# Differential-attention scores of an encoder layer on 64 contraction rows at a time, with one reduction per map

## Chip, cores and metric

One core of one Trainium2 chip runs the whole layer. The metric is the device time of one execution in microseconds (us), the median of several runs.

## What is computed

The reference is one encoder layer in float32: a norm, a wide input projection, a state-space mixer, a differential attention with 8 heads, two gates, an output projection and a feed-forward block. The change touches the scores of the attention:

```python
def one_block(args):
    qb, qpos = args
    bucket = _rel_bucket(k_pos[None, :] - qpos[:, None])
    bias = jnp.transpose(rel_table[bucket], (2, 0, 1)).astype(jnp.float32)
    s = jnp.einsum('bqhtd,bkhtd->bhtqk', qb, k,
                   preferred_element_type=jnp.float32) * scale + bias[None, :, None]
    p = jax.nn.softmax(s, axis=-1)
    w = p[:, :, 0] - lam32 * p[:, :, 1]
    return jnp.einsum('bhqk,bkhe->bqhe', w.astype(v.dtype), v)
```

There are 1024 queries, 1040 keys (16 of them from the meta tokens), 8 heads, and in each head two maps (the index t) whose head dimension is 64.

## The kernel before

Every float32 operand of a large product is split into two parts, hi and lo (`split`, line 87), and most products are made of three partial products (`mm3`, line 91): hi by hi, lo by hi, hi by lo. The program is written in a manual order, so each engine runs its instructions in the order in which the code issues them, and an instruction that waits holds up all that follow it on its engine.

The attention stage works through 64 items (8 heads by 8 query tiles of 128). Each has two maps, so there are 128 maps of 128 queries by 1040 keys. Two items make a pair. For one map the steps are these, with the names that the order tables use (m is the map, a or b the item of the pair):

- `C`, function `sc_mm`, lines 1163 and 1164, on TensorE: the keys are taken in three chunks of 352, 344 and 344 columns. The stationary operands `qa` and `qb` hold hi and lo of 64 dimensions, one above the other, in 128 rows; K holds hi above lo. `qa` by K gives hi·hi + lo·lo, `qb` by K gives the two cross terms. A chunk writes a tile `S` of its own; the pool `pps` has four of them.
- `c`, function `sc_tt`, line 1175, on VectorE: one custom instruction per chunk adds the bias table `Tb`, writes the sum to `E` and keeps a running minimum in `mn`. The second and third chunk start from the `mn` that the chunk before left, and each instruction is followed by a short one that reads the accumulator out.
- `exp` (line 1181, ScalarE), `coef` (lines 1187 and 1188, VectorE), `comb` (lines 1195 to 1198, GpSimd: the two maps become one weight matrix `w`).
- `T` (line 1204, TensorE: transposes of `w` into the PSUM tile `wt`, two of which exist), `hi` (line 1214, ScalarE) and `lo` (line 1218, VectorE: the split of the transposed weights), `PV` (line 1239, TensorE: weights by V).

Beside these, each step of the loop carries a piece of the gated linear unit of the state-space branch (`GLU`, function `glu_mm`, 12 products through lines 92 to 94 into tile `f` or `o`), a transpose and a square for the norm of the attention output (`sqT`, `sq`), and small norm steps on VectorE (`n`, lines 1268 to 1280, through `mul` at line 85). The strings `RAMP`, `STEPS` and `TAIL` (lines 1473 to 1493) are the order, written out by hand: `STEPS` is one step of the steady loop (line 1572), a list of names, each with the number of steps by which its pair lags. Loads are issued on the SP queue by `load_head` and `load_q` once per head.

```python
nc.tensor.matmul(ps[:, 0:n], qa[:, qs], k, start=True, stop=False)
nc.tensor.matmul(ps[:, 0:n], qb[:, qs], k, start=False, stop=True)
```

Of the kernel before, what the change touches and what calls it, by code (L numbers as in the profile page):

```python
# [46 lines left out]
def _f(ap):  # L47
    return ap.bitcast(F32)
# [3 lines left out]
def tile_hybrid_encoder(ctx, tc, A, out, dbg=None, stop=None):  # L52
# [973 lines left out]
    HT = {}  # L1026

    def load_q(h, p):

        if h >= H:  # L1030
            return
        c = slice(512 * p, 512 * p + 512)
        for m in range(2):
            qa, qb = [kq.tile([128, 512], F32R, tag=f"Q{z}{m}", name=f"Q{z}{m}", bufs=2) for z in range(2)]
            d = slice(64 * m, 64 * m + 64)
            for z in range(2):
                o = slice(64 * z, 64 * z + 64)
                nc.sync.dma_start(_f(qa[o]), qd[h, z, d, c])
                nc.sync.dma_start(_f(qb[o]), qd[h, 1 - z, d, c])
            HT.setdefault(h, {})["Q", p, m] = qa, qb  # L1040

    def load_head(h):
        if h >= H:
            return
        K = [kq.tile([128, L], F32R, tag=f"K{m}", name=f"K{m}_{h}") for m in range(2)]
        Tb = kq.tile([128, 896 + L], F32, tag="Tb", name=f"Tb{h}")
        load_q(h, 0)
        for m in range(2):
            for z in range(2):
                nc.sync.dma_start(_f(K[m][64 * z:64 * z + 64]), kd[h, z, 64 * m:64 * m + 64, :])  # L1050

        tr = td[h, 0:1]
        nc.sync.dma_start(Tb, bass.AP(tr.tensor, tr.offset, [[1, 128], [1, 896 + L]]))
        HT[h].update(K=K, Tb=Tb)

# [42 lines left out]
    def open_s():  # L1098

        nonlocal pps  # L1100
        PP["c"].close()
        pps = pS.enter_context(tc.tile_pool(name="pps", bufs=4, space=PSUM, side="right"))
# [44 lines left out]
    CH = ((0, 352), (352, 344), (696, 344))  # L1147

    def sc_mm(i, m, c):
# [8 lines left out]
        c0, n = CH[c]  # L1158
        ps = IT[i]["S", m, c] = pps.tile([128, 352], F32, tag="S", name="S")
        qs = slice(128 * (qt % 4), 128 * (qt % 4) + 128)  # L1160
        k = hd["K"][m][:, c0:c0 + n]
        qa, qb = hd["Q", qt // 4, m]
        nc.tensor.matmul(ps[:, 0:n], qa[:, qs], k, start=True, stop=False)  # L1163
        nc.tensor.matmul(ps[:, 0:n], qb[:, qs], k, start=False, stop=True)  # L1164

    def sc_tt(i, m, c):
# [3 lines left out]
        if c == 0:  # L1170
            t["E", m] = ptl(ep, f"E{m}", [128, L], F32, 2)
        c0, n = CH[c]
        mn = t["mn"][:, m:m + 1]
        b0 = 128 * qt + c0
        V.tensor_tensor_reduce(out=t["E", m][:, c0:c0 + n], in0=t.pop(("S", m, c))[:, 0:n],  # L1175
                               in1=HT[h]["Tb"][:, b0:b0 + n], scale=1.0,
                               scalar=mn if c else 3.0e38, op0=ALU.add, op1=ALU.min, accum_out=mn)
# [289 lines left out]
    def c_step(u, c, t):  # L1467
# [5 lines left out]
    RAMP = ("X C01a@0 C00a@0 c00a@0 c01a@0 S C10b@0 S C10a@0 c10a@0 G S G N0 C02a@0 c02a@0 exp0a@0 S S H C12a@0 "  # L1473
# [8 lines left out]
    TAIL = ("c02b@31 c lo0b@30 sqT@29 exp0b@31 lo1b@30 coefb@31 sqa@29 T2b@30 sqb@29 combb@31 PV0y@30 PV0z@30 tanh "  # L1482
# [5 lines left out]
    STEPS = ("c02b:2 lo0b:3 C11a:1 sqT:4 C12a:1 lo1b:3 c10a:1 exp0b:2 c11a:1 C00a:1 sqa:4 T2b:3 coefb:2 C01a:1 "  # L1488
# [5 lines left out]
    ACTS = {}  # L1494
    for x in range(2):
        s_ = "ab"[x]
        for m in range(2):
            ACTS[f"exp{m}{s_}"] = lambda p, m=m, x=x: ex_map(2 * p + x, m)
            for c in range(3):
                ACTS[f"C{m}{c}{s_}"] = lambda p, m=m, c=c, x=x: sc_mm(2 * p + x, m, c)  # L1500
                ACTS[f"c{m}{c}{s_}"] = lambda p, m=m, c=c, x=x: sc_tt(2 * p + x, m, c)
# [29 lines left out]
    LC = max(lag for n, lag in order if n[0] in "Cc" and n[1] in "01")  # L1531
# [593 lines left out]
```

## Time and profile before

| | |
|---|---|
| median of 3 runs | 1905.64 us (1902.81 to 1908.32) |
| the profiled execution | 1903.11 us, of which the span of its instructions is 1900.9 us |
| PE, PEld, DVE busy over the span | 96 %, 86 %, 67 % |
| ACT, POOL busy over the span | 46 %, 46 % |
| mean granted clock of TensorE | 0.989 |
| the attention stage | scores from 637.8 to 1068.1 us |

PE is TensorE's matrix multiply, PEld its weight load, DVE is VectorE, ACT ScalarE, POOL GpSimd. A row of a group gives line, engine, operation, output and inputs, the shape, the count, the busy time, the mean length of one and the idle time of the engine just before. A matmul's length in the records includes the time through the array, so records of matmuls that follow one another overlap; the distance between their starts is what one of them costs the engine.

### The profile page before, as it was taken

How to read it: one execution, taken by the hardware profiler on the slowest of the kernel's cores; microseconds unless marked ns; L12 is line 12 of the kernel's file. 1: busy time of each engine (PE TensorE's matmuls, PEld its weight loads, DVE VectorE, ACT ScalarE, POOL GpSimd, SP SyncE). 2: the span in 40 equal slices, each digit the busy share in tenths (PEclk: the TensorE clock that was granted, in tenths of full speed). 3: DMA queues.
4: the chain of work that ended last, by engine and by line, in shares of the span. 5: the costliest groups of instructions: out<-in, count | busy, mean ns of one | idle time of the engine just before them, and what ended most of it. 6: DMA issues, size and time to landing. Idle time of an engine off the chain costs nothing. (4 is left out here: it accounts for less than half of the span.)

```text
span 1900.9 us, 31037 instructions
## 1 busy us (share of the span) xinstructions
PE 1827.6 (96%) x11306; PEld 1642.2 (86%) x11306; DVE 1268.6 (67%) x2601; ACT 867.9 (46%) x1597; POOL 871.6 (46%) x803
## 2 busy tenths in 40 slices
PE   8998999899999989999999899999999999999999
PEld 7997888889999889999999888998788887888887
DVE  6699997763544688989999864369554545654543
ACT  4324343233433367777767632234555554433332
POOL 3068999643332177777767500005765652400000
PEclk8999999999999999999999999999999999999999
DMA  7423323337678565454554346431644448986563
GB/s 218 121 76 86 99 89 109 99 103 235 234 245 290 199 172 148 128 155 140 154 145 143 108 161 219 133 117 56 214 146 157 148 156 304 345 282 202 183 210 116
DMA packets 230535, 315.89 MB, mean 166 GB/s; under 512 B 39560, under 2 KB 140472, under 8 KB 230344
## 3 DMA queue, kind: packets, MB, share of 16 engines
q1 hardware_dynamic: 209952, 283.14, 47.1%
q10 hardware_dynamic: 20432, 30.78, 4.4%
q8 instruction: 89, 1.46, 0.3%
q14 instruction: 62, 0.51, 0.1%
HBM read 212.28 MB, written 99.48 MB: 164 GB/s over the span
## 5 line engine op out<-in xcount | busy, mean ns | idle before, releaser
L89 DVE TENSOR_TENSOR fp<-fr,fp 128x1024 fp32r<-128x1024 f32 x112 | 141.1, 1306 | 128.0 <-ACT fp L88 127.4
L92 PE MATMUL ps<-wh,hnh 128*128 128x256 f32 x768 | 221.3, 288 | 4.7 <-DVE qraw L969 3.5
L93 PE MATMUL ps<-wh,hnl 128*128 128x256 f32 x768 | 219.1, 285 | 4.6 <-DVE hnl L89 4.6
L94 PE MATMUL ps<-wl,hnh 128*128 128x256 f32 x768 | 218.8, 285 | 0.0
L88 ACT CAST fp<-fr 128x1024 fp32r<-128x1024 f32 x112 | 110.4, 1050 | 180.8 <-PE pf L94 159.2
L94 PE MATMUL pf<-fp 128*128 128x512 f32 x448 | 174.5, 390 | 1.3 <-DVE fp L89 1.3
L92 PE MATMUL pf<-fp 128*128 128x512 f32 x448 | 174.5, 390 | 0.5 <-ACT fp L88 0.4
L93 PE MATMUL pf<-fp 128*128 128x512 f32 x448 | 174.3, 389 | 0.0
L1181 ACT ACTIVATE E<-E,st 128x1040 f32<-128x1040 f32 x128 | 149.4, 1167 | 47.4 <-DVE st L1175 37.7
L1175 DVE CUSTOM_DVE_ANT_0 E<-S,Tb,st 128x344 f32<-128x344 f32 x256 | 146.7, 574 | 27.1 <-PE S L1164 5.7
L1197 POOL TENSOR_TENSOR w<-E,E 128x1040 f32<-128x1040 f32 x64 | 155.4, 2427 | 5.3
L92 PEld LDWEIGHTS ps<-wh,hnh 128*128 128x128 f32 x768 | 147.7, 192 | 6.9 <-DVE qraw L969 4.1
L93 PEld LDWEIGHTS ps<-wh,hnl 128*128 128x128 f32 x768 | 147.8, 192 | 4.9 <-DVE hnl L89 4.8
L94 PEld LDWEIGHTS ps<-wl,hnh 128*128 128x128 f32 x768 | 148.0, 193 | 0.0
L1163 PE MATMUL S<-K,Q 128*128 128x344 f32 (+1 forms) x384 | 134.5, 351 | 3.1 <-issue 3.0
L92 PE MATMUL ps<-hnh,wh 128*128 128x512 f32 (+2 forms) x352 | 133.6, 380 | 0.0
L93 PE MATMUL ps<-hnh,wl 128*128 128x512 f32 (+2 forms) x352 | 132.3, 376 | 1.3 <-POOL wl L174 1.0
L94 PE MATMUL ps<-hnl,wh 128*128 128x512 f32 (+2 forms) x352 | 131.4, 373 | 0.0
L89 DVE TENSOR_TENSOR swl<-w1r,swh 128x512 fp32r<-128x512 f32 x70 | 79.6, 1167 | 70.4 <-ACT swh L88 70.3
L1214 ACT CAST W<-wt 128x384 fp32r<-128x384 f32 x192 | 89.3, 481 | 79.3 <-PE wt L1204 71.6
L1164 PE MATMUL S<-K,Q 128*128 128x344 f32 (+1 forms) x384 | 123.5, 323 | 0.0
L1195 POOL TENSOR_SCALAR E<-E,st 128x1040 f32<-128x1040 f32 x64 | 74.4, 1163 | 97.1 <-DVE st L1188 55.3
(428 smaller groups left out, 5328.4 us busy)
## 6 DMA issues: line engine op xcount, KB each, us to landing
fr<-ad SPq DMA_DIRECT2D x56, 512.0 KB
ad<-r SPq DMA_DIRECT2D x91, 256.0 KB
raw<-in_w_in_dram SPq DMA_DIRECT2D x44, 512.0 KB
w<-in_w_ff_dram SPq DMA_DIRECT2D x32, 512.0 KB
wd<-w SPq DMA_DIRECT2D x32, 512.0 KB
Q<-qd SPq DMA_DIRECT2D x128, 128.0 KB
fr<-wd SPq DMA_DIRECT2D x32, 512.0 KB
w1r<-in_w_ff_dram SPq DMA_DIRECT2D x28, 512.0 KB
```

The lines of the kernel that those rows point to most:

```text
L88: nc.scalar.copy(hi, src)
L89: (eng or nc.vector).tensor_tensor(out=lo, in0=src, in1=_f(hi), op=ALU.subtract)
L92: nc.tensor.matmul(o, l[0], r[0], start=start, stop=False, **kw)
L93: nc.tensor.matmul(o, l[1], r[0], start=False, stop=False, **kw)
L94: nc.tensor.matmul(o, l[0], r[1], start=False, stop=stop, **kw)
L1163: nc.tensor.matmul(ps[:, 0:n], qa[:, qs], k, start=True, stop=False)
L1164: nc.tensor.matmul(ps[:, 0:n], qb[:, qs], k, start=False, stop=True)
L1175: V.tensor_tensor_reduce(out=t["E", m][:, c0:c0 + n], in0=t.pop(("S", m, c))[:, 0:n], in1=HT[h]["Tb"][:, b0:b0 + n], scale=1.0, scalar=mn ...
L1181: nc.scalar.activation(t["E", m], t["E", m], AF.Exp, bias=t["mn"][:, m:m + 1], scale=-1.0, accum_out=t["Z"][:, m:m + 1])
L1195: nc.gpsimd.tensor_scalar(out=E1, in0=E1, scalar1=t["cf"][:, 0:1], scalar2=0.0, op0=ALU.mult, op1=ALU.add)
L1197: nc.gpsimd.tensor_tensor(out=w[:, 112:], in0=_rev(E0), in1=_rev(E1), op=ALU.add)
L1214: nc.scalar.copy(WT[p, g][:, :, 0, x], IT[i]["tp", g])
```

## The change

The scores of a map are no longer two products over 128 rows but three over 64 rows, for two halves of the keys. Rows 0 to 63 of K hold the first 520 keys, rows 64 to 127 the last 520, in both cases hi in the first 520 columns and lo in the next 520. `qa` now holds hi in both halves of its rows and `qb` lo. A group of 260 keys gets three matmuls (hi·hi, lo·hi, hi·lo; the lo·lo term is left out), each on 64 rows and 260 columns; the groups of the upper and the lower rows alternate, so that consecutive matmuls use different halves of the array. A map has four groups and twelve matmuls. Its scores fill one tile of four banks, of which `pps` now has one instead of four small ones. VectorE runs one instruction over 1040 columns per map instead of three. K's loads read the same bytes in rows of 520 elements. `RAMP`, `STEPS` and `TAIL` are written anew; all twelve matmuls of a map now stand together.

```diff
+    NC = L // 4
@@ load_q
-                nc.sync.dma_start(_f(qa[o]), qd[h, z, d, c])
-                nc.sync.dma_start(_f(qb[o]), qd[h, 1 - z, d, c])
+                nc.sync.dma_start(_f(qa[o]), qd[h, 0, d, c])
+                nc.sync.dma_start(_f(qb[o]), qd[h, 1, d, c])
@@ load_head
-                nc.sync.dma_start(_f(K[m][64 * z:64 * z + 64]), kd[h, z, 64 * m:64 * m + 64, :])
+                nc.sync.dma_start(_f(K[m][64 * z:64 * z + 64]).rearrange("p (y n) -> p y n", y=2),
+                                  kd[h, :, 64 * m:64 * m + 64, 2 * NC * z:2 * NC * z + 2 * NC].rearrange("y p n -> p y n"))
@@ open_s
-        pps = pS.enter_context(tc.tile_pool(name="pps", bufs=4, space=PSUM, side="right"))
+        pps = pS.enter_context(tc.tile_pool(name="pps", bufs=1, space=PSUM, side="right"))
@@ sc_mm
-        c0, n = CH[c]
-        ps = IT[i]["S", m, c] = pps.tile([128, 352], F32, tag="S", name="S")
+        if c == 0:
+            IT[i]["S", m] = pps.tile([128, 4, 512], F32, tag="S", name="S")
+        if c % 2:
+            return
         qs = slice(128 * (qt % 4), 128 * (qt % 4) + 128)
-        k = hd["K"][m][:, c0:c0 + n]
         qa, qb = hd["Q", qt // 4, m]
-        nc.tensor.matmul(ps[:, 0:n], qa[:, qs], k, start=True, stop=False)
-        nc.tensor.matmul(ps[:, 0:n], qb[:, qs], k, start=False, stop=True)
+        for n, (q, y) in enumerate(((qa, 0), (qb, 0), (qa, 1))):
+            for z in range(2):
+                o = slice(64 * z, 64 * z + 64)
+                k0 = 2 * NC * y + NC * (c // 2)
+                nc.tensor.matmul(IT[i]["S", m][:, 2 * z + c // 2, 0:NC], q[o, qs], hd["K"][m][o, k0:k0 + NC],
+                                 start=n == 0, stop=n == 2)
@@ sc_tt
+        E = t["E", m] = ptl(ep, f"E{m}", [128, L], F32, 2)
+        b0 = 128 * qt
+        V.tensor_tensor_reduce(out=E.rearrange("p (c n) -> p c n", c=4), in0=t.pop(("S", m))[:, :, 0:NC],
+                               in1=HT[h]["Tb"][:, b0:b0 + L].rearrange("p (c n) -> p c n", c=4), scale=1.0,
+                               scalar=3.0e38, op0=ALU.add, op1=ALU.min, accum_out=t["mn"][:, m:m + 1])
@@ STEPS (first line of eight)
-    STEPS = ("c02b:2 lo0b:3 C11a:1 sqT:4 C12a:1 lo1b:3 c10a:1 exp0b:2 c11a:1 C00a:1 sqa:4 T2b:3 coefb:2 C01a:1 "
+    STEPS = ("C10a:1 C11a:1 C12a:1 C13a:1 lo0b:3 lo1b:3 sqT:4 exp0b:2 c1a:1 sqa:4 T2b:3 coefb:2 sqb:4 tanh:2 "
```

How the order moves is seen at two places of the steady loop. The first is TensorE, from the end of one group of PV products (line 1239 before, 1244 after the change) over a map of scores; K and Q are the operands of one map, `wt` the transposed weights. Before:

```order
L1163 MATMUL S<-K_5_10811,Q_10819 128x352 [waits DVE_49]
L1164 MATMUL S<-K_5_10811,Q_10820 128x352
L1163 MATMUL S<-K_5_10811,Q_10819 128x344 [waits DVE_49]
L1164 MATMUL S<-K_5_10811,Q_10820 128x344
L1204 MATMUL wt<-idn,w_7405 128x128 [waits DVE_49]
L1204 MATMUL wt<-idn,w_7405 128x128 x2
L1239 MATMUL o<-W,VV 128x256 x9
L1163 MATMUL S<-K_5_10811,Q_10819 128x344 [waits DVE_49]
L1164 MATMUL S<-K_5_10811,Q_10820 128x344
L1239 MATMUL o<-W,VV 128x256 [waits Activation_49]
```

With the change:

```order
L1244 MATMUL o<-W,VV 128x256 [waits Activation_49]
L1244 MATMUL o<-W,VV 128x256 x3
L1171 MATMUL S<-K_4_10172,Q_10575 128x260 [waits DVE_49]
L1171 MATMUL S<-K_4_10172,Q_10575 128x260
L1171 MATMUL S<-K_4_10172,Q_10576 128x260 x2
L1171 MATMUL S<-K_4_10172,Q_10575 128x260 x4
L1171 MATMUL S<-K_4_10172,Q_10576 128x260 x2
L1171 MATMUL S<-K_4_10172,Q_10575 128x260 x2
L1244 MATMUL o<-W,VV 128x256 x5
```

The six matmuls of a map, which stood in two or three places with transposes and PV products between them, have become a block of twelve that opens with a wait for VectorE.

The second place is VectorE over two maps of scores; `W` is the split of the transposed weights. Before:

```order
L1175 ISA E_10786,st<-S,Tb_10056 128x352 [waits PE_49]
L1175 ISA st 128x1
L1175 ISA E_10786,st<-S,Tb_10056,st 128x344 [waits DVE_49,PE_49]
L1175 ISA st 128x1
L1175 ISA E_10786,st<-S,Tb_10056,st 128x344 [waits DVE_49,PE_49]
L1175 ISA st 128x1
L1218 TENSOR_TENSOR W<-wt,W 128x3x128 [waits Activation_49] x2
L1175 ISA E_10842,st<-S,Tb_10056 128x352 [waits Pool_49]
```

With the change:

```order
L1180 ISA E_11298,st<-S,Tb_10961 128x1040 [waits PE_49,Pool_49]
L1180 ISA st 128x1
L1223 TENSOR_TENSOR W<-wt,W 128x3x128 [waits Activation_49]
L1180 ISA E_11338,st<-S,Tb_10961 128x1040 [waits PE_49]
L1180 ISA st 128x1
L1223 TENSOR_TENSOR W<-wt,W 128x3x128 [waits Activation_49] x2
L1180 ISA E_11392,st<-S,Tb_10961 128x1040 [waits PE_49,Pool_49]
```

Three instructions with two waits on VectorE's own earlier result have become one, which waits for all twelve matmuls of its map.

## Rows read from the trace of the kernel before

**Rows 1.** Busy time of each engine in the steady part of the attention stage.

```profile
core 0: us, PE busy (x) PEld busy (x) DVE busy (x) ACT busy (x) POOL busy (x), PEclk, DMA share, GB/s
700.00:1075.00 375.00, 357.35 (x2753) 348.50 (x2752) 337.73 (x1109) 268.80 (x604) 272.34 (x224) 0.99 0.49 142
760.00:1040.00 280.00, 265.82 (x2041) 259.27 (x2041) 254.44 (x828) 198.52 (x446) 202.31 (x166) 0.99 0.50 146
```

**Rows 2.** Who waited for whom, TensorE alone, 700 to 1075 us: total, times, longest.

```profile
PE wt L1204 <- DVE W L1218: 12.6, 7, 2.1
PE ot L1253 <- DVE W L1218: 4.8, 7, 1.0
PE S L1163 <- issue: 0.2, 1, 0.2
```

**Rows 3.** Groups of instructions by line from 760 to 1040 us.

```profile
L1175 DVE CUSTOM_DVE_ANT_0 E<-S,Tb,st 128x344 f32<-128x344 f32 x174 | 100.0, 574 | 18.8 <-PE S L1164 3.7
L1163 PE MATMUL S<-K,Q 128*128 128x344 f32 (+1 forms) x261 | 91.1, 350 | 0.0
L1164 PE MATMUL S<-K,Q 128*128 128x344 f32 (+1 forms) x262 | 84.0, 322 | 0.0
L1239 PE MATMUL o<-W,VV 128*128 128x256 f32 x519 | 78.1, 286 | 0.0
...
L1204 PE MATMUL wt<-idn,w 128*128 128x128 f32 x390 | 61.3, 274 | 10.8 <-DVE W L1218 10.8
...
L92 PE MATMUL f<-yTh,wh 128*128 128x256 f32 x172 | 51.4, 299 | 0.0
...
L1175 DVE CUSTOM_DVE_ANT_0 E<-S,Tb 128x352 f32<-128x352 f32 x87 | 44.9, 517 | 0.0
```

**Rows 4.** Timeline of TensorE: start, length, instruction.

```profile
963.55 0.28 PE L92 MATMUL f<-yTh,wh 128*128 128x256 f32 x1
...
964.97 0.32 PE L1163 MATMUL S<-K,Q 128*128 128x344 f32 x1
...
965.60 0.32 PE L1163 MATMUL S<-K,Q 128*128 128x352 f32 x1
...
974.61 0.49 PE L1204 MATMUL wt<-idn,w 128*128 128x128 f32 x3
```

**Rows 5.** Timeline of VectorE over one map.

```profile
962.94 0.52 DVE L1175 CUSTOM_DVE_ANT_0 E<-S,Tb 128x352 f32<-128x352 f32 x1
963.38 0.08 DVE L1175 DVE_READ_ACCUMULATOR2_ANT st<- 128x1 f32 x1
963.50 0.58 DVE L1175 CUSTOM_DVE_ANT_0 E<-S,Tb,st 128x344 f32<-128x344 f32 x1
...
964.23 0.58 DVE L1175 CUSTOM_DVE_ANT_0 E<-S,Tb,st 128x344 f32<-128x344 f32 x1
964.73 0.08 DVE L1175 DVE_READ_ACCUMULATOR2_ANT st<- 128x1 f32 x1
964.73 2.12 DVE L85 TENSOR_TENSOR ora<-ory 128x8 f32<-128x8 f32 x1
```

**Rows 6.** Timeline of TensorE where a product over 64 rows (line 731) stands alone.

```profile
69.75 0.28 PE L93 MATMUL ps<-wh,hnl 128*128 128x256 f32 x1
69.87 0.28 PE L94 MATMUL ps<-wl,hnh 128*128 128x256 f32 x1
70.08 0.39 PE L731 MATMUL pt<-oh,tr 64*8 64x512 f32 x1
70.40 0.39 PE L92 MATMUL ps<-wh,hnh 128*128 128x256 f32 x1
70.62 0.28 PE L93 MATMUL ps<-wh,hnl 128*128 128x256 f32 x1
```

**Rows 7.** Two products of 512 columns in a row, timeline of TensorE.

```profile
1499.82 0.39 PE L92 MATMUL pe<-to,swh 128*128 128x512 f32 x1
1500.04 0.39 PE L93 MATMUL pe<-to,swl 128*128 128x512 f32 x1
```

**Rows 8.** Weight loads by line: length minimum/median/maximum in ns, first and last start.

```profile
L260 PEld LDWEIGHTS ps<-wh,hm x64: 120/121/124, 18.6 to 608.2; 128*48 128x48 f32 x64
L731 PEld LDWEIGHTS pt<-oh,tr x5: 82/82/82, 48.7 to 76.3; 64*8 64x8 f32 x5
L1163 PEld LDWEIGHTS S<-K,Q x384: 186/189/330, 637.8 to 1068.0; 128*128 128x128 f32 x192
```

**Rows 9.** VectorE additions from PSUM, groups by form over the whole span.

```profile
L1218 DVE TENSOR_TENSOR W<-wt,W 128x384 fp32r<-128x384 f32 x192 | 103.2, 551 | 2.9 <-ACT W L1214 2.2
...
L2022 DVE TENSOR_TENSOR acc<-acc,pf 128x512 f32<-128x512 f32 x28 | 19.2, 685 | 30.0 <-PE pf L94 29.9
```

**Rows 10.** Small norm steps of VectorE, 760 to 1040 us: ns minimum/median/maximum.

```profile
L85 DVE TENSOR_TENSOR ora<-ory x17: 156/449/2121, 759.4 to 1025.9; 128x8 f32<-128x8 f32 x17
```

**Rows 11.** DMA queue and the loads of Q, 700 to 1075 us.

```profile
q1 hardware_dynamic: 39112, 52.88, 48.9%
Q<-qd SPq DMA_DIRECT2D x112, 128.0 KB
```

More of the change, by code (lines that the diff above doesn't have):

```diff
@@ L1146, in tile_hybrid_encoder @@
     IT = {}
-    CH = ((0, 352), (352, 344), (696, 344))
     def sc_mm(i, m, c):
@@ L1157, in sc_mm, with sc_tt @@
             IT[i] = dict(mn=st[:, 0:2], Z=st[:, 2:4], cf=st[:, 4:6])
-        c0, n = CH[c]
-        ps = IT[i]["S", m, c] = pps.tile([128, 352], F32, tag="S", name="S")
+        if c == 0:
+            IT[i]["S", m] = pps.tile([128, 4, 512], F32, tag="S", name="S")
+        if c % 2:
+            return
         qs = slice(128 * (qt % 4), 128 * (qt % 4) + 128)
-        k = hd["K"][m][:, c0:c0 + n]
         qa, qb = hd["Q", qt // 4, m]
-        nc.tensor.matmul(ps[:, 0:n], qa[:, qs], k, start=True, stop=False)
-        nc.tensor.matmul(ps[:, 0:n], qb[:, qs], k, start=False, stop=True)
-    def sc_tt(i, m, c):
+        for n, (q, y) in enumerate(((qa, 0), (qb, 0), (qa, 1))):
[4 more added lines that the diff above has]
+                                 start=n == 0, stop=n == 2)
+    def sc_tt(i, m):
         h, qt = divmod(i, NT)
         t = IT[i]
[L1170 to L1177, printed above, removed]
+        E = t["E", m] = ptl(ep, f"E{m}", [128, L], F32, 2)
[3 more added lines that the diff above has]
+                               scalar=3.0e38, op0=ALU.add, op1=ALU.min, accum_out=t["mn"][:, m:m + 1])
     def ex_map(i, m):
@@ L1472, in tile_hybrid_encoder @@
     norm = [iter(())]
-    RAMP = ("X C01a@0 C00a@0 c00a@0 c01a@0 S C10b@0 S C10a@0 c10a@0 G S G N0 C02a@0 c02a@0 exp0a@0 S S H C12a@0 "
[8 rows of a table removed]
-    TAIL = ("c02b@31 c lo0b@30 sqT@29 exp0b@31 lo1b@30 coefb@31 sqa@29 T2b@30 sqb@29 combb@31 PV0y@30 PV0z@30 tanh "
+    RAMP = ("X C00a@0 C01a@0 C02a@0 C03a@0 S S G S G N0 c0a@0 exp0a@0 S S H C10a@0 C11a@0 C12a@0 C13a@0 G c1a@0 "
[7 rows of a table added]
+    TAIL = ("c lo0b@30 sqT@29 exp0b@31 lo1b@30 coefb@31 sqa@29 T2b@30 sqb@29 combb@31 PV0y@30 PV0z@30 tanh "
             "hi2b@30 lo2b@30 T0a@31 n PV1y@30 PV1z@30 n T1a@31 hi0a@31 lo0a@31 d hi1a@31 lo1a@31 n n n post PV2y@30 "
@@ L1498, in tile_hybrid_encoder @@
             ACTS[f"exp{m}{s_}"] = lambda p, m=m, x=x: ex_map(2 * p + x, m)
-            for c in range(3):
+            ACTS[f"c{m}{s_}"] = lambda p, m=m, x=x: sc_tt(2 * p + x, m)
+            for c in range(4):
                 ACTS[f"C{m}{c}{s_}"] = lambda p, m=m, c=c, x=x: sc_mm(2 * p + x, m, c)
-                ACTS[f"c{m}{c}{s_}"] = lambda p, m=m, c=c, x=x: sc_tt(2 * p + x, m, c)
         for n, f in (("T", w_T), ("hi", w_hi), ("lo", w_lo)):
@@ L1530, in tile_hybrid_encoder @@
     lag_of = dict(order)
-    LC = max(lag for n, lag in order if n[0] in "Cc" and n[1] in "01")
+    LC = 2
     LP, LS = lag_of["PV2z"], max(lag_of["sqa"], lag_of["sqb"])
```

25 rows, old and new, of tables (RAMP, STEPS) are left out of this document.

## Prediction

> **What bounds the kernel now.** I read the stage in which the change lies first. Over its steady part, 700 to 1075 us, PE is busy 357 of 375 us and DVE 338 [rows 1]; ACT and POOL have a quarter of their time free. A busy PE in the records is not yet a full one, so I counted what its products cost by the distance between starts. Twelve products of 256 columns take 963.55 to 964.97, 0.118 us each; four score products of 344 columns take 964.97 to 965.60, 0.158 each; three transposes take 0.49 where one is 0.27 long, 0.11 apart [rows 3, 4]. From 760 to 1040 us there are 523 score products, 519 PV products, 3 times 172 of the linear unit and 390 transposes [rows 3]: 82.6 + 61.2 + 60.9 + 42.9 = 248 us of 280, and smaller groups fill some of the rest. DVE is tighter still: 254.4 us busy in the same 280 [rows 1], and 18.8 idle before the second and third chunk of a map, of which PE accounts for 3.7 [rows 3]; the other 15.1 go to its wait for its own running minimum. That makes 269.5 of 280, 96 %. So DVE sets the pace and PE is close behind. The waits say the same: of what PE loses in 700 to 1075 us, 12.6 + 4.8 = 17.4 us are waits for DVE's split of the transposed weights, which holds the two `wt` tiles [rows 2], and almost nothing else is listed.
>
> A pair of items has four maps; 87 first chunks in 280 us [rows 3] are 21.75 pairs, 12.9 us each.
>
> **DVE: three instructions become one.** A map now takes from 962.94 to 964.73, 1.79 us [rows 5]. One instruction over 1040 columns has no row. The first chunk takes 0.517 for 352 columns [rows 3]; two additions from PSUM give 685 - 551 = 134 ns for 128 more columns, 1.05 ns each [rows 9]; 0.517 + 688 x 1.05 ns = 1.24 us, and its read-out ends where the next would begin. That frees 0.55 us per map, 70 us in 128 maps, and brings DVE to about 80 % of the stage. None of this is time by itself: it counts as far as PE waited for DVE, at most the 17.4 us. I take **-15**.
>
> **PE: fewer columns, if two halves run together.** Before, a map costs 6 x 0.158 = 0.95 us. A product of 260 columns costs, between the two rows above, 0.12 us. Twelve of them in pairs, one on the upper and one on the lower rows, cost 6 x 0.12 = 0.72 if a pair takes the time of one, and 12 x 0.12 = 1.44 if the halves take turns. No row of this trace has two products on different rows, so these are the two ends: -0.23 or +0.49 us per map, -29 or +62 us in 128 maps. I take the first, **-29**: the two products of a pair share no rows of the array, no K columns and no PSUM bank, and nothing in the order puts a wait between them.
>
> The Trainium skill's page "TensorE: Matmul & The Clock Gate" (Part 3: Packing small matmuls) says that products in different row groups run at the same time, with starts about 4 ns apart; no run here shows it yet.
>
> **PE: the way into and out of the half array.** This is the cost that the description of the change doesn't show. A product on 64 rows stands alone between full ones at line 731 [rows 6]. From the full product before it (69.87) to the second one behind it (70.62) pass 0.75 us. At the usual distances, 0.118 + 0.22 (512 columns, [rows 7]) + 0.118, it would be 0.46. So one visit costs 0.29 us more than its columns. Its weights have 8 columns, and their load is 0.08 long; the scores' load has 128 columns and is 0.19 long [rows 8]. If that load can't start before the full products are through, a visit costs 0.29 + 0.11 = 0.40. I take 0.35, halfway. In the new order every map is one block between transposes, PV products and products of the linear unit, all on 128 rows: one visit per map, 128 x 0.35 = **+45** (37 to 51).
>
> **A new wait.** The scores had four small tiles, so PE could run ahead of DVE. Now one tile holds all four banks: a block can't start before DVE has read the map before it. Behind its last product come about 0.16 us (length 0.32 less distance 0.16, [rows 4]) until the result is there and 1.24 on DVE, some 1.4 to 1.5 with the hand-over. Between the blocks PE has, by the new `STEPS`, 8 transposes and 8 PV products (1.8 us), 3 and 13 (1.9), 6 transposes, 5 PV products and 12 of the linear unit (2.7), 3 transposes and 12 of the linear unit (1.7). All four cover the wait if DVE is free when the scores are done. But DVE may be inside a 0.55 us split [rows 9], or in a small norm step that takes 0.16 us at best and up to 2.12 [rows 10], and three of the four gaps have only 0.3 to 0.4 to spare. I take 0.1 us per block, **+13**; the bounds are 0 and 0.3, +38. Behind PE's wait stand the transposes, and behind those ACT and POOL, which have room.
>
> **Loads.** K's bytes are the same in twice as many pieces, on the same queue, in the same place of the order, once per head and more than a step ahead. The queue's packets fill 49 % of the engines in the stage, with the Q loads among them [rows 11]. I cost that at nothing; the cover is the step of 12.9 us by which the loads lead.
>
> **Sum**, against the profiled execution (1903.1): -15 - 29 + 45 + 13 = +14, so 1917. The median of the runs, 1905.6, is 2.5 above that execution, so against it the change is +11, 0.6 %. With the bounds of the visit and of the new wait this case spans 1896 (-15 - 29 + 37) to 1948 (-15 - 29 + 51 + 38).
>
> **Rival 1: the halves take turns.** Then a map costs 12 x 0.12 instead of 6 x 0.158: +62 + 45 - 15 + 13 = +105, **2008**. A milder form is that only the weight loads take turns. A load of 48 columns is 0.121 long, one of 128 is 0.189 [rows 8]: 0.85 ns per column, so about 0.11 us for 128 columns, and the number of loads rises from 6 to 12 per map. 12 x 0.11 = 1.32 instead of 0.95 is +47 instead of -29: +47 + 45 - 15 + 13 = +90, **1993**. Against it: nothing in the trace, which has no such pair; for it: each load of the scores lies under a product now, and twelve short ones would have less to lie under. Here the change doesn't do what it says.
>
> The Trainium skill's page "TensorE: Matmul & The Clock Gate" (LDWEIGHTS) gives a load as its columns over 1.2, whatever the rows, 107 ns for 128 columns. [Rows 8] agree, with 109 by the slope. By its figure twelve loads in turn would be an estimated 1.28 us per map, 1988 in all.
>
> **Rival 2: in between.** Pairs overlap in part, at 0.17 us a pair: 6 x 0.17 = 1.02, +9 instead of -29, so +52, **1955**.
>
> **Rival 3, faster: the visit costs little.** If the first load of a block and the first behind it slip under the products before them, as loads do inside the full array now, the visit falls to about 0.05 us: -29 + 6 - 15, and a new wait of +8 because DVE and PE both have more room: -30, **1873**. With no visit cost it is 1867. It decides from 0.24 us per visit: there the four terms sum to nothing. Against it stands the one row with 64 rows, with 0.29, which had a load of only 8 columns.
>
> **Chances.** The forecast 0.45, rival 1 0.25, rival 2 0.13, rival 3 0.17. A measurement of this kernel can tell about 0.3 %, 5.7 us, from no change: the bounds are 1899.9 and 1911.4. Faster takes all of rival 3 and a tenth of the forecast, 0.22; the same takes three tenths of the forecast, 0.14; slower is the rest, 0.64. The likeliest case alone holds 1896 to 1948. The range reaches down to rival 3 at 1868 and up to 1985, which takes in rival 2 and the lower edge of rival 1 (its milder form with a cheap visit and no new wait); the rest of rival 1, about two in ten, is left out.
>
> **What would show it.** Right: two score records of one pair start a few ns apart, blocks of twelve last about 0.75 us from first to last start, the full products around a block stand 0.3 to 0.4 us further from it than before, DVE falls under 82 % in the stage, its waits behind PE's transposes are gone, and PE waits before line 1171 for line 1180 about 10 us in all. Wrong: score records 0.11 to 0.12 us apart (rival 1); blocks that begin 0.12 us after a full product (rival 3); waits for line 1180 of over 40 us, which would make the single tile the cause and not the array.

## The result, and the profile after the change

The changed kernel takes 1921.97 us (median; 1920.78 to 1932.10 over four runs) against 1905.11 (1902.81 to 1908.32) for the kernel before in runs beside it. The ratio is 1.0099, with a 95 % interval of 1.0069 to 1.0128: it is slower, by about 17 us. The profiled execution took 1922.69 us. Below, 0.001 of a ratio is 1.9 us, and medians are compared unless a ratio is given.

First the page of the changed kernel: busy time of each engine, and the groups of the new VectorE instruction and of the score products (busy time, mean ns of one | idle time before them, and what ended it).

```profile
PE 1847.9 (96%) x12074; PEld 1627.6 (85%) x12074; DVE 1223.2 (64%) x2089; ACT 867.3 (45%) x1597; POOL 867.2 (45%) x803
...
L1180 DVE CUSTOM_DVE_ANT_0 E<-S,Tb 128x1040 f32<-128x1040 f32 x128 | 158.7, 1240 | 78.8 <-PE S L1171 73.6
...
L1171 PE MATMUL S<-K,Q 64*128 64x260 f32 x1536 | 128.5, 299 | 8.2 <-DVE st L1180 5.2
```

The one instruction lasts 1.24 us, as forecast, and DVE now idles 78.8 us in front of it, nearly all of it for PE's scores. DVE is no longer the engine that sets the pace. The busy times of the two stretches of [rows 1] say the same, with DVE at 217 of 280 us (78 %) where it was 254:

```profile
700.00:1075.00 375.00, 359.24 (x3351) 321.71 (x3349) 284.88 (x613) 260.18 (x583) 265.27 (x218) 1.00 0.49 142
...
760.00:1040.00 280.00, 267.72 (x2490) 239.68 (x2488) 217.04 (x468) 192.74 (x434) 196.83 (x162) 1.00 0.51 149
```

TensorE's waits from 700 to 1075 us, the counterpart of [rows 2] (total, times, longest):

```profile
PE wt L1209 <- ACT ot L1264: 9.3, 28, 0.3
PE S L1171 <- DVE st L1180: 4.3, 7, 0.9
PE yt L1291 <- DVE W L1223: 2.2, 6, 0.4
```

The 17.4 us of waits of [rows 2] for DVE's split are gone (2.2 us of such waits stand at line 1291). All waits recorded now make 15.8 us: 4.3 us are the wait of a block of scores for the single tile, as foreseen, and 9.3 us are a wait that the prediction does not name, of the transposes for ScalarE's square (`sqa`).

**The block of a map.** Timeline of TensorE in the changed kernel (start, length, instruction, count of a run of like records, idle time before it). L92 to L94 are the linear unit, L1171 the scores, L1209 the transposes.

```profile
901.68 0.28 PE L93 MATMUL f<-yTh,wl 128*128 128x256 f32 x1
901.80 0.28 PE L94 MATMUL f<-yTl,wh 128*128 128x256 f32 x1
902.01 0.99 PE L1171 MATMUL S<-K,Q 64*128 64x260 f32 x12
902.93 0.55 PE L1209 MATMUL wt<-idn,w 128*128 128x128 f32 x3
903.23 0.36 PE L92 MATMUL f<-yTh,wh 128*128 128x256 f32 x1
903.43 0.27 PE L93 MATMUL f<-yTh,wl 128*128 128x256 f32 x1
...
907.31 0.52 PE L1209 MATMUL wt<-idn,w 128*128 128x128 f32 x3 [0.33 <-ACT ot L1264]
```

From 901.80 to 903.43 pass 1.63 us. One product of the linear unit before the block (0.12), three transposes (0.33) and one more product (0.12) belong to others; 1.06 us are the block's. The block is a typical one: over all 128 blocks the medians are 0.21 us from the last product on 128 rows to the first score product, 0.71 from the first start to the last, and 0.21 to the next product on 128 rows. The forecast was 0.72 + 0.35 = 1.07; before, a map cost 0.95. When the window is opened later and later, the same run of twelve loses its records two at a time:

```profile
902.23 0.76 PE L1171 MATMUL S<-K,Q 64*128 64x260 f32 x10
...
902.71 0.28 PE L1171 MATMUL S<-K,Q 64*128 64x260 f32 x2
```

Two products start together, and the pairs stand 0.12 us apart: the halves do run at the same time. The Trainium skill's page "TensorE: Matmul & The Clock Gate" (Part 3: Packing small matmuls) says so, and these rows agree. The weight loads of the same block show where a part of the other 0.34 us goes:

```profile
901.68 0.19 PEld L94 LDWEIGHTS f<-yTl,wh 128*128 128x128 f32 x1
902.00 0.18 PEld L1171 LDWEIGHTS S<-K,Q 64*128 64x128 f32 x2
...
902.60 0.19 PEld L1171 LDWEIGHTS S<-K,Q 64*128 64x128 f32 x2
902.92 0.31 PEld L1209 LDWEIGHTS wt<-idn,w 128*128 128x128 f32 x3
```

In the full array a load begins with the product before its own: L94's at 901.68, as L93 starts. The first load of the block begins at 902.00, 0.20 us after the last full product started, and the first load behind it at 902.92, 0.21 us after the last pair (902.71). At both ends the load begins some 0.2 us behind the start of the last product instead of with it. The Trainium skill's page "TensorEngine Tiling (Array Packing)" (Key Properties) says that a change of tiling mode drains the engine, without a price; these rows agree. The two ends, 0.21 where products usually stand 0.12 apart, make 0.18 of the 0.34 us; 0.10 more lie between the first pair (902.01) and the second (902.23), the rest in the transposes behind the block.

**Steady part and start.** A map's first VectorE instruction is a mark for progress. Counted along the timeline, the 33rd and the 121st map begin here, in the kernel before and in the changed one:

```profile
765.05 0.52 DVE L1175 CUSTOM_DVE_ANT_0 E<-S,Tb 128x352 f32<-128x352 f32 x1
...
1046.60 0.52 DVE L1175 CUSTOM_DVE_ANT_0 E<-S,Tb 128x352 f32<-128x352 f32 x1
```

```profile
773.33 1.24 DVE L1180 CUSTOM_DVE_ANT_0 E<-S,Tb 128x1040 f32<-128x1040 f32 x1 [0.30 <-issue]
...
1065.35 1.24 DVE L1180 CUSTOM_DVE_ANT_0 E<-S,Tb 128x1040 f32<-128x1040 f32 x1 [0.73 <-PE S L1171]
```

For 88 maps that is 281.55 us before and 292.02 after, 0.119 us more per map. But the 33rd map is already 8.3 us late, of which 32 x 0.119 = 3.8 us are this rate: about 4.5 us are lost at the start of the stage, of which the prediction says nothing. The granted clock differs there too: between 636 and 695 us TensorE has 17.0 us at its lower level (0.50) in the changed kernel and 6.8 us in the kernel before. At that level products of the linear unit start 0.21 us apart instead of 0.12 (shown under e9), so 10.2 us more of it are an estimated 4.6 us where TensorE is what limits: as much as is missing.

### The profile page after: what moved, and what is told of

It reads as the page before. It is cut to its first block, busy times and chain, and to the rows that moved or that the text cites. A ratio compares the mean times of both kernels' runs of the same rounds, so it can differ in the third digit from the quotient of the medians.

```text
span 1920.9 us, 31806 instructions
## 1 busy us (share of the span) xinstructions
PE 1847.9 (96%) x12074; PEld 1627.6 (85%) x12074; DVE 1223.2 (64%) x2089; ACT 867.3 (45%) x1597; POOL 867.2 (45%) x803
## 5 line engine op out<-in xcount | busy, mean ns | idle before, releaser
L93 PE MATMUL ps<-wh,hnl 128*128 128x256 f32 x768 | 217.7, 283 | 5.3 <-DVE hnl L89 5.2
L92 PE MATMUL ps<-wh,hnh 128*128 128x256 f32 x768 | 220.0, 286 | 2.8 <-DVE qraw L969 1.6
L94 PE MATMUL ps<-wl,hnh 128*128 128x256 f32 x768 | 217.4, 283 | 0.0
L1180 DVE CUSTOM_DVE_ANT_0 E<-S,Tb 128x1040 f32<-128x1040 f32 x128 | 158.7, 1240 | 78.8 <-PE S L1171 73.6
L94 PE MATMUL pf<-fp 128*128 128x512 f32 x448 | 174.5, 390 | 1.3 <-DVE fp L89 1.3
L92 PE MATMUL pf<-fp 128*128 128x512 f32 x448 | 174.5, 390 | 0.6 <-ACT fp L88 0.6
L93 PE MATMUL pf<-fp 128*128 128x512 f32 x448 | 174.3, 389 | 0.0
L93 PEld LDWEIGHTS ps<-wh,hnl 128*128 128x128 f32 x768 | 146.3, 190 | 5.8 <-DVE hnl L89 5.8
L92 PEld LDWEIGHTS ps<-wh,hnh 128*128 128x128 f32 x768 | 146.2, 190 | 5.3 <-DVE qraw L969 2.2
L94 PEld LDWEIGHTS ps<-wl,hnh 128*128 128x128 f32 x768 | 146.3, 191 | 0.0
L1171 PE MATMUL S<-K,Q 64*128 64x260 f32 x1536 | 128.5, 299 | 8.2 <-DVE st L1180 5.2
L92 PE MATMUL ps<-hnh,wh 128*128 128x512 f32 (+2 forms) x352 | 135.6, 385 | 0.0
L93 PE MATMUL ps<-hnh,wl 128*128 128x512 f32 (+2 forms) x352 | 133.4, 379 | 1.2 <-POOL wl L174 1.0
L94 PE MATMUL ps<-hnl,wh 128*128 128x512 f32 (+2 forms) x352 | 132.3, 376 | 0.0
L1171 PEld LDWEIGHTS S<-K,Q 64*128 64x128 f32 x1536 | 101.7, 188 | 27.1 <-DVE st L1180 7.4
L1244 PE MATMUL o<-W,VV 128*128 128x256 f32 x768 | 123.5, 295 | 0.0
```

What stands on the lines that cost most here:

```text
L92: nc.tensor.matmul(o, l[0], r[0], start=start, stop=False, **kw)
L93: nc.tensor.matmul(o, l[1], r[0], start=False, stop=False, **kw)
L94: nc.tensor.matmul(o, l[0], r[1], start=False, stop=stop, **kw)
L1171: nc.tensor.matmul(IT[i]["S", m][:, 2 * z + c // 2, 0:NC], q[o, qs], hd["K"][m][o, k0:k0 + NC], start=n == 0, stop=n == 2)
L1180: V.tensor_tensor_reduce(out=E.rearrange("p (c n) -> p c n", c=4), in0=t.pop(("S", m))[:, :, 0:NC], in1=HT[h]["Tb"][:, b0:b0 + L].rearrang ...
L1244: nc.tensor.matmul(PO[p], v, w, start=g == 0 and n == 0, stop=g == 2 and n == 8)
```

## The experiments

The theory: a visit of half the array costs some 0.35 us per map and outweighs the columns saved, and the rest comes from waits that the new order makes. The rivals: the single tile is the cause, or the whole loss is the order's.

### e1: the scores on 128 rows again, the new order kept

```diff
-        for n, (q, y) in enumerate(((qa, 0), (qb, 0), (qa, 1))):
...
+        ps, k = IT[i]["S", m][:, c, 0:NC], hd["K"][m][:, NC * c:NC * c + NC]
+        nc.tensor.matmul(ps, qa[:, qs], k, start=True, stop=False)
+        nc.tensor.matmul(ps, qb[:, qs], k, start=False, stop=True)
```

With the scores the layout of the loads of K and Q also goes back to that of the kernel before.

> The changed kernel with the scores on 128 rows again: hi above lo, two products per group, four groups of 260 columns, in the same order, with the same single tile of four banks and the one VectorE instruction per map. Theory V (a visit of the half array costs 0.34 us per map and outweighs the columns it saves): a block falls from 1.06 us (6 x 0.12 + 0.34) to 8 x 0.12 = 0.96, 128 x -0.10 = -13, so about 1909 where the change has 1922, and the gap before a block of scores is gone. Rival W (the single tile and the longer VectorE step make PE wait, whatever the rows): about 1922, no change. Rival O (the new order makes the transposes wait for ScalarE's square): about 1922 too, with the same 0.3 us waits before the transposes.

Measured: 1911.97 us, ratio 1.0041 (1.0027 to 1.0055): 10 us less than the changed kernel. Timeline of TensorE, the first and the last of the eight products of a block with their neighbours:

```profile
932.83 0.28 PE L94 MATMUL f<-yTl,wh 128*128 128x256 f32 x1
932.95 0.28 PE L1165 MATMUL S<-K,Q 128*128 128x260 f32 x1
...
933.79 0.28 PE L1166 MATMUL S<-K,Q 128*128 128x260 f32 x1
933.91 0.49 PE L1203 MATMUL wt<-idn,w 128*128 128x128 f32 x3
```

No gap at either end: 8 x 0.12 = 0.96 us against 1.06, which by itself would be 13 us in 128 maps. The halves (with their layout of the loads, which no run separates) cost time, but 7 us remain that they do not explain.

### e2: the first transposes behind both PV products

```diff
-             "PV0y:3 T0a:2 wla:0 PV0z:3 hi2b:3 lo2b:3 exp1a:1 C00a:1 C01a:1 C02a:1 C03a:1 mulq:1 T1a:2 n3a:3 "
+             "PV0y:3 wla:0 PV0z:3 T0a:2 hi2b:3 lo2b:3 exp1a:1 C00a:1 C01a:1 C02a:1 C03a:1 mulq:1 T1a:2 n3a:3 "
```

> The changed kernel with one step moved: PV0z stands before T0a, so TensorE has 0.6 us of products before the transpose that now waits 0.33 us for ScalarE's square of the attention output, 28 times, 9.3 us in all. Rival O: the wait goes, -6 to -9, about 1914. Theory V: the waits are a part beside the visits and only that part comes back, at most -9. Rival W: nothing, 1922, because the time is in the wait for the single tile.

Measured: 1911.49 us, ratio 1.0040 (1.0023 to 1.0056), 10.5 us less. TensorE's waits from 700 to 1075 us:

```profile
PE S L1171 <- DVE st L1180: 6.8, 8, 1.0
```

The wait for ACT is gone (that of L1291 stands as it was). `sqT` writes its tile `ot` into a buffer of the same pool as `wt` (two buffers), so `T0a` needs that one back, and ACT must first have read the square from it. Before, score products stood between; the change took them away, and the 0.33 us once per pair came bare: 32 x 0.33 = 10.6 us. That this equals the gain is not a proof by itself, since the wait for the single tile grew from 4.3 to 6.8 us. The steady rate says the same, though: from the 33rd to the 121st map 284.22 us instead of 292.02, 0.089 us per map, 11 us in 128.

### e3 and e8: a second visit, and its control

```diff
+        if c == 2:
+            nc.tensor.matmul(IT[i]["S", m][:, 0, 300:316], qa[:, qs], hd["K"][m][:, 0:16], start=True, stop=True)
```

e3 puts one short product on all 128 rows into the middle of each block of the changed kernel; e8 puts the same one into the blocks of e1.

> The changed kernel with one product of 16 columns on all 128 rows put into the middle of each block of twelve (it writes columns of the tile that nobody reads), so each map visits the half array twice. Its own columns cost 0.03 us or less. Theory V: one more visit per map, 128 x (0.34 + 0.03) = +47, about 1969. Rivals W and O, and the view that the twelve weight loads and not the change of rows cost the time: +0.03 to 0.12 per map, 4 to 15 us, 1926 to 1937.

> The kernel of e1 (scores on 128 rows) with the same extra product as e3: 16 columns on 128 rows, in the middle of each block, into columns that nobody reads. Here nothing changes the rows in use, so if the 48 us of e3 are the second visit of half the array, this run is about 128 x 0.03 us = 4 us above e1: 1912 + 4 = 1916 us, and the extra product starts some 0.03 to 0.12 us ahead of the next. Rival: the extra product itself (its weight load, its place in the order) is what cost 48 us in e3: then about 1960 us here, and the price of the visit is not known from e3.

Measured: e3 1970.36 us, ratio 1.0344 (1.0326 to 1.0361), 48 us above the changed kernel. e8 1924.24 us, ratio 1.0098 (1.0075 to 1.0122), 12 us above e1: more than the 4 expected, since the short product takes a place of its own in the row. So the second visit costs 48 - 12 = 36 us, 0.28 us each. Timeline of TensorE in e3:

```profile
932.71 0.63 PE L1173 MATMUL S<-K,Q 64*128 64x260 f32 x6
933.27 0.28 PE L1168 MATMUL S<-K,Q 128*128 128x16 f32 x1
933.48 0.63 PE L1173 MATMUL S<-K,Q 64*128 64x260 f32 x6
934.04 0.55 PE L1211 MATMUL wt<-idn,w 128*128 128x128 f32 x3
```

From the first score product to the transposes pass 1.33 us, 0.92 in the changed kernel (902.01 to 902.93). In e8 the short product (L1165) adds 0.12: from 930.01 to 930.37 it makes three steps of two.

```profile
930.01 0.29 PE L1168 MATMUL S<-K,Q 128*128 128x260 f32 x1
930.14 0.17 PE L1165 MATMUL S<-K,Q 128*128 128x16 f32 x1
930.17 0.37 PE L1167 MATMUL S<-K,Q 128*128 128x260 f32 x1
930.37 0.28 PE L1168 MATMUL S<-K,Q 128*128 128x260 f32 x1
```

1.33 - 0.92 - 0.12 = 0.29 us. The price of the visit is shown twice, by the times of the runs and by the rows.

### e4: first the upper half, then the lower

```diff
-        for n, (q, y) in enumerate(((qa, 0), (qb, 0), (qa, 1))):
-            for z in range(2):
...
+        for z in range(2):
+            o = slice(64 * z, 64 * z + 64)
+            for b in range(2):
+                for n, (q, y) in enumerate(((qa, 0), (qb, 0), (qa, 1))):
```

> The changed kernel with the same twelve products per map, but the six of the upper rows first and then the six of the lower rows, so that only one pair of neighbours lies on different rows. Theory V takes it that the alternating order makes pairs run together: 11 slots of 0.12 us instead of 6, +0.60 per map, +77, about 1999, with score products 0.12 us apart instead of in pairs. If the order of the halves doesn't matter (the array runs ahead on its own, or pairs never overlapped): 1922.

Measured: 1962.14 us, ratio 1.0300 (1.0285 to 1.0315), 40 us above the changed kernel, half of what was expected. Timeline of TensorE, one run of twelve, the window opened ever later:

```profile
931.88 1.33 PE L1172 MATMUL S<-K,Q 64*128 64x260 f32 x12
932.10 1.11 PE L1172 MATMUL S<-K,Q 64*128 64x260 f32 x11
932.22 0.99 PE L1172 MATMUL S<-K,Q 64*128 64x260 f32 x10
932.23 0.98 PE L1172 MATMUL S<-K,Q 64*128 64x260 f32 x9
932.34 0.86 PE L1172 MATMUL S<-K,Q 64*128 64x260 f32 x8
```

Alternating the halves matters: the block takes 0.34 us more (931.88 to 933.14 against 0.92). But it is not eleven places of 0.12, as an order kept strictly would give; the last section comes back to this.

### e5 and e7: e1 and e2 together; then the bias row later too

e5 makes both edits; e7 also moves `bcT` behind `PV2y`:

```diff
-             "hi0a:2 c0a:1 PV1y:3 hi1a:2 combb:2 lo0a:2 PV1z:3 bcT:3 n2b:4 PV2y:3 post:2 exp0a:1 lo1a:2 n3b:4 "
+             "hi0a:2 c0a:1 PV1y:3 hi1a:2 combb:2 lo0a:2 PV1z:3 n2b:4 PV2y:3 bcT:3 post:2 exp0a:1 lo1a:2 n3b:4 "
```

> Both single edits at once: scores on 128 rows (1912 alone) and PV0z ahead of T0a (1911.5 alone, from 1922), with the single tile and the one VectorE instruction kept. Theory: the two are separate places on TensorE, so their gains add: 1922 - 10 - 10.5 = about 1901.5, ratio to the kernel before about 0.998. If the two gains are the same time seen twice (TensorE then waits elsewhere), about 1911.

> The kernel of both edits, and the small transpose of the norm row (bcT, once per head) put behind PV2y, since it waited 0.5 us for VectorE's split six times, 3.0 us in all. Theory: -2 to -3 beside the kernel of both edits, about 1899; if the wait only moves to the next transpose, no difference.

Measured: e5 1906.16 us, ratio 1.0011 (1.0001 to 1.0022); e7 1904.37, ratio 1.0005 (0.9996 to 1.0015). The two gains of 10 us make 16 together, not 20: with less in TensorE's way, it waits longer in front of the single tile (8.0 us from 700 to 1075 us in e5, 4.9 in e1, 6.8 in e2). e7 is level with the kernel before.

### e6: three VectorE instructions again, on the single tile

```diff
+        for c0, c1 in ((0, 1), (1, 2), (2, 4)):
...
+                                   scalar=mn if c0 else 3.0e38, op0=ALU.add, op1=ALU.min, accum_out=mn)
```

> The kernel of both edits, with the merge on VectorE undone: three chained instructions per map again (260, 260 and 520 columns), everything else kept. Theory: VectorE's work per map rises by about 0.55 us to some 1.8, its share of the stage from about 80 to about 95 %, and the waits for it come back: 128 x 0.55 = 70 us of work, of which 10 to 25 us show, 1912 to 1927. If VectorE has room enough either way: within 3 us of the kernel of both edits.

Measured: 1956.05 us, ratio 1.0285 (1.0264 to 1.0305), 50 us above e5: a miss, twice the upper bound. VectorE's groups from 700 to 1075 us in e6:

```profile
L1177 DVE CUSTOM_DVE_ANT_0 E<-S,Tb,st 128x520 f32<-128x520 f32 x105 | 79.7, 759 | 3.8
L1177 DVE CUSTOM_DVE_ANT_0 E<-S,Tb,st 128x260 f32<-128x260 f32 x104 | 50.9, 489 | 3.7
L1177 DVE CUSTOM_DVE_ANT_0 E<-S,Tb 128x260 f32<-128x260 f32 x105 | 44.6, 425 | 48.3 <-PE S L1166 42.3 <-issue 6.0
```

0.43 + 0.49 + 0.76 = 1.67 us per map where one instruction takes 1.24: 0.43 more, 55 us in 128 maps, and nearly all of it is time. DVE still idles 48.3 us in front of the first instruction, 42.3 of it for the scores. With one tile neither engine can run ahead of the other: scores, minimum and the next scores are a chain, and what the minimum takes is in it. The expectation had priced it as busy time of an engine with room. The chain is not all: of the 34 us that TensorE waits from 700 to 1075 us, 20 are in front of scores and 14 for the split, and from 834 to 1070 us its granted clock falls to the lower level four times, 13.6 us in all, which it does not in e5. By the estimate under e9 that is about 6 of the 50 us.

### e9: two tiles of half a map, two VectorE instructions

```diff
-        pps = pS.enter_context(tc.tile_pool(name="pps", bufs=1, space=PSUM, side="right"))
+        pps = pS.enter_context(tc.tile_pool(name="pps", bufs=2, space=PSUM, side="right"))
...
+        for y in range(2):
```

> The kernel of e7 with S as two tiles of two banks each and two DVE instructions of 520 columns per map, chained through st, so that PE may write the first half of the next map while DVE still reads the second half of this one. If the single tile is what PE still waits for in e7, its waits for DVE in front of the scores go (some 8 us in the stretch 640 to 1110 us) and the DVE pays about 128 x 0.2 us = 26 us of its own idle time: 1896 to 1902 us, ahead of both kernels. Rival: DVE's time per map, with the extra instruction, comes into the chain from scores to minimum to next scores as in e6: then 1905 to 1920 us.

Measured: 1916.97 us, ratio 1.0063 (1.0048 to 1.0078), 12.6 us above e7. TensorE's waits from 700 to 1075 us:

```profile
PE wt L1207 <- DVE W L1221: 13.3, 6, 2.2
PE S L1165 <- DVE st L1177: 0.2, 1, 0.2
```

The waits in front of the scores are gone, as expected (7.9 us in e7), and the split holds up the transposes again with 13.3 us, much as in [rows 2]: a second instruction per map brings DVE to 319 of 375 us and the wait for it back. But all recorded waits together are only 4.2 us longer than in e7 (13.5 against 9.3). Most of the rest goes with TensorE's granted clock. Between 769 and 1088 us it falls to its lower level five times, 17 us in all, each time around the end of a wait of 2.2 us for the split (of seven such waits two pass without it); in e7 it doesn't fall there. One of the five, the transposes behind the wait and then the busy times of the stretch that follows (as in [rows 1]: the clock is the third figure from the end):

```profile
925.72 0.55 PE L1207 MATMUL wt<-idn,w 128*128 128x128 f32 x3 [2.21 <-DVE W L1221]
```

```profile
927.00:930.00 3.00, 3.00 (x16) 3.00 (x15) 2.50 (x8) 1.26 (x2) 0.00 (x0) 0.50 0.00 0
```

The kernel before does the same at two of three such waits in its steady part, at 813 and at 916 us, 6.8 us in all. Its TensorE after the first:

```profile
813.41 0.56 PE L1204 MATMUL wt<-idn,w 128*128 128x128 f32 x3 [2.11 <-DVE W L1218]
...
813.98 0.41 PE L93 MATMUL f<-yTh,wl 128*128 128x256 f32 x1
814.19 0.41 PE L94 MATMUL f<-yTl,wh 128*128 128x256 f32 x1
```

Products there start 0.21 us apart instead of 0.12, so a microsecond at the lower level loses an estimated 0.45: 7.6 us in e9 and 3 in the kernel before. With the 4.2 us of waits that is 11.8 of e9's 12.6. So what the second instruction costs here is the wait for the split and, with it, the clock.

### e10, e11, e12: the start of the stage, and the array alone

```diff
-    RAMP = ("X C00a@0 C01a@0 C02a@0 C03a@0 S S G S G N0 c0a@0 exp0a@0 S S H C10a@0 C11a@0 C12a@0 C13a@0 G c1a@0 "
+    RAMP = ("X C00a@0 C01a@0 C02a@0 C03a@0 c0a@0 S S G S G N0 exp0a@0 S S H C10a@0 C11a@0 C12a@0 C13a@0 G c1a@0 "
```

e10 is e7 with this, e11 the changed kernel with this alone, and e12 is e10 with the changed kernel's scores on 64 rows.

> The kernel of e7 with one step of the order moved, at the start of the stage: VectorE's minimum of the first map directly behind its scores, ahead of the scaling of the next Q and of the weights' split. In e7 the steady part already runs 0.037 us per map ahead of the kernel before (278.3 against 281.55 us for 88 maps), and what eats it is the start: the first minimum of a map starts 7.2 us later than before (645.98 against 638.81) and the 33rd 5.0 later. If it is the place of that minimum in the order which delays the start, 2 to 5 us come back: 1899 to 1902 us, ahead of both kernels. Rival: the start is set by the loads of K and Q and by TensorE's lower granted clock in 638 to 644 us, not by the minimum: then 1904 as e7.

> The changed kernel with the same step moved at the start of the stage, nothing else. Its 33rd map starts 8.3 us later than before (773.33 against 765.05), of which the steady difference of 0.119 us per map explains 3.8. If the place of the first minimum is what costs the rest, 2 to 4 us come back: 1918 to 1920 us. Rival: the start does not depend on it: 1922 us, as the changed kernel.

> The kernel of e10 with the scores of the changed kernel: three products on 64 rows, halves together, and its layout of K and Q; order, single tile and the one VectorE instruction are those of e10. It tells what the array part alone is worth in an order that no longer hides or adds anything. A block of twelve cost 1.06 us and a block of eight 0.96: +0.10 us per map, +13 us, less what e10's waits in front of the scores can take up (8 us in the stretch 700 to 1075 us): 1905 to 1912 us, that is 5 to 13 us behind e10 and, by the sum, 4 to 11 us ahead of the changed kernel with the first minimum earlier (1916). Rival: the waits of the order were what cost, not the array: then 1900 us as e10.

Measured: e10 1899.48 us, ratio 0.9976 (0.9962 to 0.9990), faster than both kernels. e11 1916.00, ratio 1.0054 (1.0041 to 1.0068), 6 us below the changed kernel, more than expected. e12 1905.72, ratio 1.0008 (0.9998 to 1.0017), 6 us above e10.

The first minima on VectorE's timeline, in the changed kernel and in e11:

```profile
644.32 1.23 DVE L1180 CUSTOM_DVE_ANT_0 E<-S,Tb 128x1040 f32<-128x1040 f32 x1
647.57 1.24 DVE L1180 CUSTOM_DVE_ANT_0 E<-S,Tb 128x1040 f32<-128x1040 f32 x1 [2.01 <-PE S L1171]
```

```profile
635.84 1.24 DVE L1180 CUSTOM_DVE_ANT_0 E<-S,Tb 128x1040 f32<-128x1040 f32 x1 [1.31 <-PE S L1171]
643.59 1.23 DVE L1180 CUSTOM_DVE_ANT_0 E<-S,Tb 128x1040 f32<-128x1040 f32 x1
```

In the changed kernel the first minimum stood behind other work of VectorE, and the second block of scores needs its tile. In e11 the 33rd map starts at 767.19 instead of 773.33. Most of that need not be the order's: TensorE's granted clock was at its lower level (0.50) in the changed kernel from 638 to 642 us,

```profile
638.00:642.00 4.00, 4.00 (x14) 3.09 (x12) 3.59 (x13) 0.62 (x1) 0.00 (x0) 0.50 0.00 0
```

and 1.00 there in the kernel before and in e11. Just ahead of it TensorE had idled 3.04 us for the first scores, 2.73 in the kernel before. From 636 to 695 us the changed kernel has 17.0 us at the lower level and e11 6.8: by the estimate under e9 about 4.6 of the 6.1 us by which the 33rd map is earlier. In e10, with 10.2 us there against 13.6 in e7, it is about 1.5 of 3.8 us. The other executions agree: the span times the share of the clock that was not granted is 23 us in the changed kernel and 18 in e11 (means of four and six), 21 in e7 and 19 in e10 (of twelve and six). That leaves about 2 us for the place of the first minimum. Whether its place also moves the clock is not shown: in e1, e2, e5 and e7, which have the changed kernel's order at the start, the stretch at the lower level around 638 us lasts between nothing (e5) and 6.8 us (e7).

TensorE's waits for the single tile from 700 to 1075 us in e10, then in e12:

```profile
PE S L1165 <- DVE st L1174: 6.2, 13, 1.0
```

```profile
PE S L1171 <- DVE st L1180: 6.6, 7, 1.0
```

With two smaller groups (1.7 us for a load, 1.4 for the split) e10 waits 9.3 us, e12 only 6.6: a part of the dearer blocks fills gaps that e10 has anyway. These 2.7 us do not make up the whole distance from 13 to 6; where the rest is absorbed was not found. The steady rates give 4 of the 6: 278.35 us from the 33rd to the 121st map in e10 and 281.22 in e12, 0.033 us per map. So the array part, with its layout of the loads, costs 6 us here and 10 in the order of e1.

## Why the prediction was right in its sum, step by step

Slower by 11 us against the median was forecast, and 17 came. The steps fared unequally.

- **Columns in pairs (-29): held.** Pairs start together, 0.12 us apart. Rivals 1 and 2 fall with that: no record shows the halves taking turns.
- **The visit (+45, 0.35 us each): held.** 0.34 in the block's rows, 0.28 to 0.29 in e3 with its control. The load does wait at both ends; rival 3 (0.05) falls. What was added for a load of 128 columns (0.06) does not show in e3, whose visit costs the 0.29 of [rows 6]. With the columns the block came to 1.06 us against 1.07 forecast. As time the array part costs 6 to 10 us (e12, e1), not 16: by the rows a block costs 0.10 us more than e1's eight full products, 13 us in 128 maps, and some of that falls where TensorE would wait anyway.
- **DVE's relief (-15): the mechanism held, the account did not.** The instruction takes 1.24 us, and the waits behind the split went; e9 brings them back for 13.3 us. But what TensorE no longer waited for there it waited for elsewhere: 15.8 us of recorded waits after, 17.6 before. The row to ask had been which wait is second in line. What did come back is clock, which the prediction left out: from 700 to 1075 us the kernel before has 6.8 us at the lower level behind waits of 2.11 us, an estimated loss of 3 us, and the changed kernel none.
- **The single tile (+13): too large.** 4.3 us are recorded in the changed kernel, 6 to 8 in e2, e5, e7 and e10. It grows as other waits go. What remains of relief, single tile and order together is the gain of e10 over the kernel before, 4.6 us by the ratio; the granted clock alone can explain it: the span times the share of the clock not granted is 23 us in the kernel before and 19 in e10 (means of twelve and six executions).
- **The order: the step that was missing.** The prediction read from `STEPS` how much TensorE has between the blocks, but not what else the moved score products had been covering: the buffer of `ot` in front of `T0a` (10.5 us, e2), and the place of the first minimum at the start (6 us in e11, most of which goes with the granted clock). It looked at the start of the stage not at all.
- **Loads (0):** nothing spoke against it. In the waits of the steady part of the changed kernel no score waits for K or Q. In e1 and e10, with the old layout, scores wait twice, 1.7 to 1.8 us in all, for a load that the profile names as that of `ggt`, a tile that they do not read; which load it was stays open.

By the runs: from the kernel before to e10 -5 us, from e10 to e12 (the array part alone) +6, from e12 to the changed kernel (the order of three steps) +16, of which an estimated 3 us are granted clock at the start (10.2 us at the lower level in e12, 17.0 in the changed kernel). The forecast had -2, +16 and 0. The direction and the price of a visit were worked out and held; that the sum came so near was luck: what the order uncovered, costed at nothing, about made up for an array part priced too dear.

## What to carry to other kernels

Packing two halves of the array has to pay for the way in and out, here about 0.3 us per visit (both ends together), two and a half products of 256 columns. A block of twelve saves 0.24 us against e1's eight full products (0.72 against 0.96) and pays 0.34; an estimate from these numbers puts the break-even at some 17 half products in a row. When a block of work is drawn together in a hand-written order, look at every place it leaves: what stood there hid waits, and they come bare. And when an engine is relieved, look which wait is next on the engine that waited for it, before the relief is counted as time, and look at the granted clock behind the longest waits. With a single buffer between two engines, as in e6, time added to one can become time of the whole although neither is busy throughout.

## What the hardware did that had not been expected

**Products of the two halves do not start in program order.** In e4 the six products of the upper half stand ahead of the six of the lower. The third and the fourth start are 932.22 and 932.23. The rows do not name the half, but two products of one half stand 0.12 us apart in every other row; so the fourth start should be the first product of the lower half, three places ahead of the upper half's last. The waits in the trace say the same of the weight loads. In the blocks that are the first to use newly loaded keys and queries, the wait that stands on the second load of a block in the changed kernel, for the first product of the lower half, stands on the fifth load in e4; by the order of the code it would be the seventh. So the order of issue does not hold strictly on TensorE between the two halves. From the first to the last start (931.88 to 932.93) the twelve fill about nine places of 0.12 us, where strict order would need eleven and the changed kernel's pairs take six (0.71). How far ahead it can reach was not tried.

**A short product is not cheap.** A product of 16 columns between others of 260 took 0.12 us of the row in e8, as much as one of 260. Its own distance to the next start is 0.03 us (930.14 to 930.17); the start after that comes 0.20 later instead of 0.12.
